# Streaming encoder layer on one core: the sample's high and low parts as one stationary block of 64 columns, logit rows of 544 and 640 columns cut in halves, row norms spread in three copies, rope tables written by GpSimd

## The chip, the cores and the metric

The kernel runs on one core of a Trainium2 chip. The metric is the device time of one execution in microseconds; the kernel before takes 1721.83 us in the median of three runs. The engines are TensorE (PE; its weight load is PEld), VectorE (DVE), ScalarE (ACT), GpSimd (POOL) and SyncE (SP), whose queue issues nearly all DMAs.

## What is computed

One layer over 1024 prompt tokens and 32 sample tokens, which share the weights; the sample also has 512 cached keys and values for each head. Cut to what matters here:

```python
z = einsum('bld,de->ble', rmsnorm(x, g_mix), w_in)        # q, k, v of A and B, indexer, gates
q_a, k_a = rope(rmsnorm(q_a, g_qn)), rope(rmsnorm(k_a, g_kn))
q_i, k_i = rope(q_i), rope(k_i)
score = einsum('bqhl,bqh->bql', relu(einsum('bqhd,bld->bqhl', q_i, k_i)), w_i)
_, idx = top_k(where(admissible, score, -inf), topk)      # 256 keys; for the sample 136 of 544
o_a = softmax over the selected keys of q_a k_a / 8, times v_a
o_b = stick-breaking weights of sigmoid(q_b k_b / 8), strictly causal, times v_b
h = x + (sigmoid(g_A) * (o_A @ W_bA) + sigmoid(g_B) * (o_B @ W_bB)) @ W_out
y = h + relu(rmsnorm(h) @ W_up)**2 @ W_down
```

All is float32 with float32 accuracy. For that, most operands are held as a high part and a low part (the names end in h and l), both in a rounded 32-bit format that TensorE multiplies fast, and a product is the sum of three: high times high, high times low and low times high.

## The kernel before

**Order.** The program is not issued as it is written. Every instruction is recorded by a planner (class Plan), which gives it a cost and a rank (FAST, PREP, MAIN, FILL, SLOW) and emits all engines' instructions in the order of its own simulated time. So each engine has one fixed order, and nearly all instructions carry the line of that emission, line 431. Tiles are named in the trace by what they hold, and in orders a number tells tiles of one name apart.

**Stages.** Index projection (0 to about 76 us), the spreading of the row norms (`spread_rs`), projection of mixer B with the index scores beside it, the top-k search by bits (until about 330 us), projection of mixer A (`project_a`, about 300 to 460), attention B (483 to 700), attention A (700 to 910), merge and feed-forward to the end.

**Sample rows.** Tokens are handled in nine blocks of rows: eight of 128, and block NEW of the 32 sample tokens. In `index_projection` (parts 0 and 1, 328 and 256 columns) and in `project_a` (four times, 256 columns) the tokens are TensorE's stationary operand (`xh`, `xl`) and the weights stream past. Each of eight slices of the inner dimension takes three matmuls. Block NEW takes as many as a full block: 24, with 32 stationary columns. The bank `s` or `pj` that they fill is then read by `ta` and `tb` on DVE, which rotate the rows with the rope tables `tabc` and `tabs`.

**Logit rows.** In `attend`, query block t has 128(t+1) keys, in pieces of at most 512 columns (`s<-k,q`, for the high and the low part of q). Block t = 4 has 640, cut into 512 and 128. `index_scores` cuts the same way (`s<-kih,qi`, `s<-kil,qi`), and the sample there has 512 cached and 32 new keys. `attend_new` computes the sample's 544 logits for four heads at a time, at four places of the program: for each head, two matmuls over the 512 cached keys `kc` (128 stationary columns, tile `qz`) and two over the 32 new keys `kn`. `kn` is loaded for four heads by one DMA; `kc` comes from the cache through `k<-ckb` or `k<-cka`, an ACT copy and a POOL subtraction, into a ring of three tiles that the keys `k` of `attend` and the new values `vn` use too.

**Small things.** `spread_rs` writes nine 128x128 tiles (`rsb`) on POOL, each a row norm spread over a row, and transposes them on TensorE. `rope_tables` makes `tabc` and `tabs` by four products on DVE at the start of `project_a`. The constants `tri`, `tri4` and a copy of the identity are made at the start of the program.

Of the kernel before, what the change touches and what calls it, by code (L numbers as in the profile page):

```python
# [21 lines left out]
KB = D // 128  # L22
# [22 lines left out]
GATES_BESIDE = (1,1,1,1,1,1,0,0)  # L45
# [9 lines left out]
def rows(s):  # L55

    return DEC if s == NEW else 128

# [392 lines left out]
class Layer:  # L451
# [74 lines left out]

    def x_of(self, k, cs):
# [7 lines left out]
    def run(self):  # L535
# [33 lines left out]
        self.ones = c([128, 128], F32, "ones")  # L569
        nc.vector.memset(self.ones, 1.0)  # L570
        self.ident = c([128, 128], F32, "ident")
        self.identr = c([128, 128], F32R, "identr")
        self.trir = c([128, 128], F32R, "trir")
# [13 lines left out]
        for i, n in enumerate((W1, T - W1)):  # L587
            self.xh.append(nc.tile(xp, [128, KB, n], F32R, f"xh{i}"))
            self.xl.append(nc.tile(xp, [128, KB, n], F32R, f"xl{i}"))
# [99 lines left out]
        self.ft = nc.tile(rp, [128, FWORDS], F32, "ft")  # L689
        self.turn = cycle(["pj", "a", "b", "c"])  # L690
# [11 lines left out]
    def constants(self):  # L702
        nc, a = self.nc, self.a
        for name, dst, n in (("tri", self.trir, 128), ("tri4", self.tri4r, DEC)):
            st = nc.tile(self.wpool, [128, 512], F32, name, tag="wst", bufs=3)
            nc.sync.dma_start(st[:, :n], a[name])
            nc.scalar.copy(dst, st[:, :n])
        nc.scalar.copy(self.identr, self.ident)
        nc.sync.dma_start(self.gf, a["g_ffn"])

    def normalise(self, sl):
# [4 lines left out]
        for hf in range(2):  # L716
# [7 lines left out]
            for kk in range(4):  # L724
# [36 lines left out]
    def index_setup(self):  # L761
# [9 lines left out]
        self.iw = [[None] * KB, None]  # L771

# [16 lines left out]
    def index_projection(self, part, s):  # L789
# [4 lines left out]
        if self.iw[part] is None:  # L794
# [7 lines left out]
            nc.scalar.copy(self.kih[:, T:], kc)  # L802
            nc.vector.tensor_sub(self.kil[:, T:], kc, self.kih.bitcast(F32)[:, T:])
# [4 lines left out]
        for k in range(KB):  # L808
            xh, xl = self.x_of(k, ts_)
            wh, wl = ws[k]  # L810
# [998 lines left out]
```

## Time and profile before

| | |
|---|---|
| median of three runs | 1721.83 us (1721.07 to 1722.91) |
| the profiled execution | 1724.92 us, of it the span of the profile 1723.0 us |
| mean granted TensorE clock | 0.997 |
| PE busy | 1691.1 us, 98% |
| DVE, ACT, POOL busy | 1346.7, 952.8, 854.2 us |
| share of the chain of work that ended last | PE 87%, DVE 6%, DMA 3% |

The profiled execution is one of its own, 0.2% above the median. Matmuls overlap: one of 272 columns has a duration of 0.29 us in the trace, while the next starts 0.125 us behind it. So what a matmul costs in a stream is read from the distance of starts. Where the timeline puts several into one row, the next row's start ends the last of them.

### The profile page before, as it was taken

Reading aid. Unit: us, or ns where it says so; the run is one execution under the profiler, and the core shown is the slowest. Engines: PE = TensorE matmul, PEld = TensorE weight load, DVE = VectorE, ACT = ScalarE, POOL = GpSimd, SP = SyncE. Lnnn points to the kernel's source line nnn. Section 1 sums busy time; section 2 is a strip of 40 time slices with the busy share of each in tenths; the row PEclk is TensorE's granted clock in tenths of the full one; section 3 lists DMA queues with packets and bytes.
Section 4 is the critical chain, followed back from the end, with each engine's and each line's share of the span. In section 5 each row is a group of like instructions: output and inputs, shape, how many; then the busy total and the mean of one; then the engine's idle time right before and its main releaser. Section 6 shows DMA issues by size and latency. Waiting matters only on the chain.

```text
span 1723.0 us, 34981 instructions
## 1 busy us (share of the span) xinstructions
PE 1691.1 (98%) x12356; PEld 1606.2 (93%) x12356; DVE 1346.7 (78%) x2773; ACT 952.8 (55%) x2023; POOL 854.2 (50%) x703
## 2 busy tenths in 40 slices
PE   7999999999999999999999999999999999999998
PEld 7988999899989899988999999999999999989998
DVE  8666899988568778775765648999988888797756
ACT  7455788765357768886655446333333444425431
POOL 5533331344367777365568757533333456556420
PEclk9999999999999999999999999999999999999999
DMA  7234453354673646686874643534443587756744
GB/s 255 82 100 126 128 161 116 89 151 139 172 207 101 172 103 173 177 243 190 243 213 148 179 135 116 165 135 152 136 153 132 189 286 245 266 169 232 255 127 149
DMA packets 182527, 289.08 MB, mean 168 GB/s; under 512 B 30800, under 2 KB 62128, under 8 KB 182352
## 3 DMA queue, kind: packets, MB, share of 16 engines
q1 hardware_dynamic: 182064, 286.50, 54.1%
q8 instruction: 98, 1.61, 0.4%
q14 instruction: 77, 0.63, 0.1%
q10 hardware_dynamic: 288, 0.34, 0.1%
HBM read 193.59 MB, written 93.07 MB: 166 GB/s over the span
## 4 chain that ended last, share of the span: by engine, by line
PE 87%; DVE 6%; DMA 3%; issue 1%; ACT 1%; POOL 1%; SPq 0%; DVEq 0%; ACTq 0%; POOLq 0%
PE pj L431 35%; PE s L431 11%; PE c L431 11%; PE b L431 10%; PE a L431 10%; PE t L431 5%; PE o L431 4%; DMA q<-dq 1%; DMA k<-cka 1%; DVE y L431 1%; DVE junk L431 1%; DVE us L431 1%; DVE mh L431 1%; DVE xl L431 1%; DMA xt<-x 0%
## 5 line engine op out<-in xcount | busy, mean ns | idle before, releaser
L431 POOL TENSOR_TENSOR wl<-wst,wh 128x512 fp32r<-128x512 f32 x160 | 229.5, 1440 | 231.0 <-ACT wh L431 172.3
L431 PE MATMUL pj<-xl,wh 128*128 128x272 f32 (+2 forms) x1200 | 336.4, 314 | 0.0
L431 PE MATMUL pj<-xh,wh 128*128 128x272 f32 (+1 forms) x768 | 253.3, 330 | 0.4 <-ACT sq L431 0.4
L431 PE MATMUL pj<-xh,wl 128*128 128x272 f32 (+1 forms) x768 | 252.6, 329 | 0.0
L431 PEld LDWEIGHTS pj<-xl,wh 128*128 128x128 f32 x1200 | 213.3, 189 | 11.4
L431 ACT CAST wh<-wst 128x512 fp32r<-128x512 f32 x213 | 131.1, 620 | 140.6 <-PE pj L431 23.4
L431 PEld LDWEIGHTS pj<-xh,wh 128*128 128x128 f32 x768 | 145.2, 189 | 11.5 <-ACT sq L431 0.7
L431 PEld LDWEIGHTS pj<-xh,wl 128*128 128x128 f32 x768 | 145.0, 189 | 10.5
L431 POOL TENSOR_TENSOR p<-p,rem 128x383 f32<-128x383 f32 (+8 forms) x66 | 110.7, 1697 | 31.8 <-DVE rem L431 25.1
L431 DVE TENSOR_TENSOR tt<-t,tt 128x512 fp32r<-128x512 f32 (+2 forms) x168 | 100.1, 620 | 33.2 <-ACT tt L431 32.7
L431 POOL TENSOR_TENSOR wl<-y,wh 128x512 fp32r<-128x512 f32 x49 | 72.9, 1490 | 96.1 <-ACT wh L431 93.0
L431 DVE TENSOR_TENSOR_SCAN rem<-rem 128x384 f32<-128x384 f32 (+8 forms) x66 | 110.6, 1696 | 9.7 <-ACT rem L431 9.6
L431 ACT CAST tt<-t 128x512 fp32r<-128x512 f32 (+2 forms) x168 | 85.8, 539 | 40.8 <-PE t L431 37.5
L431 ACT CAST wh<-y 128x512 fp32r<-128x512 f32 x79 | 49.1, 621 | 106.1 <-issue 23.0
L431 ACT CAST wh<-us 128x512 fp32r<-128x512 f32 x64 | 39.7, 622 | 114.6 <-PE pj L431 27.6
L431 PE MATMUL o<-tt,v 128*128 128x256 f32 (+1 forms) x640 | 99.0, 280 | 3.9 <-ACT tt L431 3.5
L431 ACT ACTIVATE junk<-score,cand 128x1024 bf16<-128x1024 f32 (+2 forms) x93 | 96.9, 1042 | 9.7 <-DVE cand L431 8.4
L431 PE MATMUL s<-k,q 128*128 128x512 f32 (+3 forms) x384 | 100.7, 357 | 1.3 <-DMA q<-dq 1.0
L431 PEld LDWEIGHTS o<-tt,v 128*128 128x128 f32 x640 | 91.8, 191 | 9.9 <-ACT tt L431 4.1
L431 DVE TENSOR_SCALAR_CACHE_REDUCE junk<-score,cand 128x384 bf16<-128x384 f32 (+1 forms) x124 | 92.9, 749 | 3.1
L431 PE MATMUL t<-ident,p 128*128 128x128 f32 (+1 forms) x596 | 91.0, 276 | 0.8 <-POOL p L431 0.6
L431 POOL TENSOR_TENSOR wl<-us,wh 128x512 fp32r<-128x512 f32 x33 | 50.3, 1533 | 71.3 <-ACT wh L431 71.3
(359 smaller groups left out, 5666.5 us busy)
## 6 DMA issues: line engine op xcount, KB each, us to landing
us<-w_down SPq DMA_DIRECT2D x80, 256.0 KB, 3.1
q<-dq SPq DMA_DIRECT2D x64, 256.0 KB, 4.9
du<-y SPq DMA_DIRECT2D x56, 264.0 KB, 2.5
du<-us SPq DMA_DIRECT2D x56, 264.0 KB, 2.5
y<-w_up SPq DMA_DIRECT2D x44, 256.0 KB, 2.7
k<-dk SPq DMA_DIRECT2D x40, 256.0 KB, 5.0
v<-dv SPq DMA_DIRECT2D x40, 256.0 KB, 4.4
xl<-du SPq DMA_DIRECT2D x35, 264.0 KB, 5.3
```

Source lines behind the costliest of these rows:

```text
L431: fn(*args, **kw)
```

## The change

1. `xh` of the second half of the tokens gets 32 more columns, filled by one ACT copy with the low parts of the sample. High and low parts so stand side by side as 64 stationary columns, and block NEW takes 16 matmuls in place of 24 (`token_rows`). The lower 32 rows of the result hold the low parts' products: one ACT copy and one DVE addition (`join`) add them to the upper rows, once in each of the six places.
2. Rows of 640 and 544 logits are cut into halves of 320 and 272 (`cut`). In `attend_new` the new keys stand behind the cached ones in the tile `kc`: 16 DMAs of 16 KB, one for each head, take the place of four for `kn`. The indexer's keys stand in the same order, the sample's cached ones ahead of its new ones.
3. `spread_rs` makes its tiles by three DVE copies in place of nine POOL instructions.
4. The four rope-table products go from DVE to POOL.
5. `tri`, `tri4` and the identity copy are made just ahead of attention B, and one gate is computed beside head 6 and not beside head 5.

```diff
-GATES_BESIDE = (1,1,1,1,1,1,0,0)
+GATES_BESIDE = (1,1,1,1,1,0,1,0)
...
+def cut(L):
+
+    return L // 2 if L in (640, LS) else 512
...
+    def token_rows(self, ps, s, ws):
+
+        mm = self.nc.tensor.matmul
+        if s == NEW:
+            for k in range(KB):
+                x = self.xh[1][:, k, SEQ - W1:]
+                for i in range(2):
+                    mm(ps[:2 * DEC], x, ws[k][i], start=k + i == 0, stop=k + i == KB)
+            return
+        for k in range(KB):
+            xh, xl = self.x_of(k, slice(128 * s, 128 * s + 128))
+            mm(ps, xh, ws[k][0], start=k == 0, stop=False)
+            mm(ps, xh, ws[k][1], start=False, stop=False)
+            mm(ps, xl, ws[k][0], start=False, stop=k == KB - 1)
+
+    def join(self, ps, low):
+
+        self.nc.scalar.copy(low, ps[DEC:2 * DEC])
+        self.nc.vector.tensor_add(ps[:DEC], ps[:DEC], low)
...
-            self.xh.append(nc.tile(xp, [128, KB, n], F32R, f"xh{i}"))
+            self.xh.append(nc.tile(xp, [128, KB, n + i * DEC], F32R, f"xh{i}"))
...
+        self.trir, self.identr = (nc.tile(self.att, [128, 128], F32R, z) for z in ("trir", "identr"))
+        nc.scalar.copy(self.identr, self.ident)
+        for name, dst, n in (("tri", self.trir, 128), ("tri4", self.tri4r, DEC)):
+            st = nc.tile(self.att, [128, 512], F32, name, tag="gz", bufs=3)
+            nc.sync.dma_start(st[:, :n], a[name])
+            nc.scalar.copy(dst, st[:, :n])
...
+        if sl[-1] == NEW:
+            nc.scalar.copy(self.xh[1][:, :, T - W1:], self.xl[1].bitcast(F32)[:, :, SEQ - W1:])
...
+            b = nc.tile(self.pr, [128, 2, 512], F32R, "rsb", tag="zz", bufs=2).bitcast(F32)[:, 0]
+            b = b.rearrange("p (t e) -> p t e", e=128)[:, :len(sl)]
+            nc.vector.tensor_copy(b, self.rs[:, sl[0]:sl[-1] + 1].unsqueeze(2).to_broadcast([128, len(sl), 128]))
             for i, s in enumerate(sl):
-                b = nc.tile(self.ip, [128, 5 * HD], F32, "rsb", tag="ta", bufs=2)[:, :128]
-                nc.gpsimd.tensor_scalar(b, self.ones, self.rs[:, s:s + 1], None, op0=ALU.mult)
                 m = rows(s)
-                nc.tensor.transpose(pt[:, i * 128:i * 128 + m], b[:m], self.ident[:m, :m])
+                nc.tensor.transpose(pt[:, i * 128:i * 128 + m], b[:m, i], self.ident[:m, :m])
...
-        for k in range(KB):
-            xh, xl = self.x_of(k, ts_)
-            wh, wl = ws[k]
-            nc.tensor.matmul(ps[:m, :n], xh, wh[:, :n], start=k == 0, stop=False)
-            nc.tensor.matmul(ps[:m, :n], xh, wl[:, :n], start=False, stop=False)
-            nc.tensor.matmul(ps[:m, :n], xl, wh[:, :n], start=False, stop=k == KB - 1)
+        self.token_rows(ps[:, :n], s, [[z[:, :n] for z in w] for w in ws])
+        if s == NEW:
+            self.join(ps[:, :n], nc.tile(self.wpool, [128, 512], F32, "pl", tag="wst", bufs=3)[:DEC, :n])
...
-        if t < 8:
-            L = 128 * (t + 1)
-            return [(c, min(512, L - c), c) for c in range(0, L, 512)]
-        return [(0, PAST, T), (PAST, DEC, SEQ)]
+        L = 128 * (t + 1) if t < 8 else LS
+        n = cut(L)
+        return [(c, min(n, L - c), c + (SEQ if t == 8 else 0)) for c in range(0, L, n)]
...
-            nc.vector.tensor_mul(self.tc_[:, :, j], C, g[:, j].unsqueeze(1).to_broadcast([128, NT, HD]))
+            nc.gpsimd.tensor_mul(self.tc_[:, :, j], C, g[:, j].unsqueeze(1).to_broadcast([128, NT, HD]))
...
+            self.token_rows(ps[:, :256], s, [
+                [u[:, i * 256:i * 256 + 256] for u in unit] for unit in units for i in range(2)])
+            if s == NEW:
+                self.join(ps[:, :256], nc.tile(pr, [128, 4, HD], F32, "pl", tag="sq", bufs=1).rearrange("p h e -> p (h e)")[:DEC])
...
-            for c0 in range(0, L, 512):
-                n = min(512, L - c0)
+            for c0 in range(0, L, cut(L)):
+                n = min(cut(L), L - c0)
...
-        kn = nc.tile(at, [128, 4, DEC], F32R, "kn", bufs=1)
-        nc.sync.dma_start(kn.bitcast(F32), self.dk[g0:g0 + 4, :, :, new].rearrange("j s e t -> (s e) j t"))
         for j in range(4):
             if j % 2 == 0:
                 k32 = nc.tile(at, [64, 2, PAST], F32, "k32", **(dict(tag="p", bufs=6) if is_a else dict(tag="rem", bufs=4)))
                 nc.sync.dma_start(k32, a["ck" + sfx][4 * u + j:4 * u + j + 2].rearrange("j e t -> e j t"))
-            k = nc.tile(at, [128, SEQ], F32R, "kc", tag="k", bufs=3)[:, :PAST]
-            nc.scalar.copy(k[:HD], k32[:, j % 2])
-            nc.gpsimd.tensor_sub(k[HD:], k32[:, j % 2], k.bitcast(F32)[:HD])
+            k = nc.tile(at, [128, SEQ], F32R, "kc", tag="k", bufs=3)[:, :LS]
+            nc.sync.dma_start(k.bitcast(F32)[:, PAST:], self.dk[g0 + j, :, :, new].rearrange("s e t -> (s e) t"))
+            nc.scalar.copy(k[:HD, :PAST], k32[:, j % 2])
+            nc.gpsimd.tensor_sub(k[HD:, :PAST], k32[:, j % 2], k.bitcast(F32)[:HD, :PAST])
             for i in range(2):
                 q, first, last = qq[:, i, 128 * j:128 * j + 128], j + i == 0, j + i == 4
-                nc.tensor.matmul(ps0, q, k, start=first, stop=last)
-                nc.tensor.matmul(ps1[:, :DEC], q, kn[:, j], start=first, stop=is_a and last)
+                nc.tensor.matmul(ps0[:, :LS // 2], q, k[:, :LS // 2], start=first, stop=last)
+                nc.tensor.matmul(ps1[:, :LS // 2], q, k[:, LS // 2:], start=first, stop=is_a and last)
...
-        parts = [(0, ps0[:, :]), (PAST, ps1[:, :DEC])]
+        parts = [(0, ps0[:, :LS // 2]), (LS // 2, ps1[:, :LS // 2])]
```

The planner lays the whole program out anew. Three places show it. The first is PE's order in the index projection, where block NEW's part 0 begins (`ih` and `il` are the high and low weights, `rr` and `kd` rotated rows to be transposed); before:

```order
L431 MATMUL s<-ih_128,xh_108 32x328
L431 MATMUL s<-il_129,xh_108 32x328
L431 MATMUL t<-ident,rr 128x128 x2
L431 MATMUL s<-ih_128,xl_109 32x328
L431 MATMUL s<-ih_130,xh_108 32x328
L431 MATMUL t<-ident,kd 128x128
L431 MATMUL s<-il_131,xh_108 32x328
L431 MATMUL s<-ih_130,xl_109 32x328
```

And on the same engine at the same place in the changed kernel:

```order
L436 MATMUL s<-ih_126,xh_105 64x328
L436 MATMUL s<-il_127,xh_105 64x328
L436 MATMUL s<-ih_128,xh_105 64x328
L436 MATMUL s<-il_129,xh_105 64x328
L436 MATMUL s<-ih_131,xh_105 64x328
L436 MATMUL s<-il_132,xh_105 64x328
```

The matmuls with `xl` are gone, and the result has 64 rows.

The second place is PE's order early in `project_a`, where the third part of the first values `vt` (32 columns at the end) is transposed, and further on the first rotated rows `qk`; before:

```order
L431 MATMUL pj<-xl_109,wh_1883 128x272
L431 MATMUL pj<-xh_108,wl_1884 128x272
L431 MATMUL t<-ident,vt 128x128 x2
L431 MATMUL t<-ident,vt 32x128
L431 MATMUL pj<-wh_1886,xh_108 128x256
...
L431 MATMUL pj<-wh_3889,xl_109 128x256
L431 MATMUL t<-ident,qk 128x128 x4
L431 MATMUL pj<-xh_106,wh_3946 128x512
```

The changed kernel's PE at that place:

```order
L436 MATMUL pj<-xl_106,wh_1802 128x272
L436 MATMUL pj<-xh_105,wl_1803 128x272
L436 MATMUL s<-wh_1805,xh_105 128x256
...
L436 MATMUL s<-wh_1808,xl_106 128x256
L436 MATMUL t<-ident,vt 128x128 x2
L436 MATMUL t<-ident,vt 32x128
L436 MATMUL pj<-wh_1805,xh_105 128x256
...
L436 MATMUL s<-wl_3872,xh_105 64x256
L436 MATMUL t<-ident,qk 128x128 x5
L436 MATMUL pj<-xh_103,wh_3929 128x512
```

Before, the transposes of `vt` stand directly behind the last matmul of their block, and those of `qk` 24 matmuls behind them. Now 12 matmuls of 256 columns stand ahead of the transposes of `vt`, and some 100 matmuls between them and those of `qk`.

The third place is SP's queue ahead of `attend_new` for the first four heads of mixer A; before:

```order
L431 DMA q<-dq 64x2x512 x2
L431 DMA wst<-w_bb 128x512
L431 DMA gz<-dg 128x512
L431 DMA kn<-dk 128x4x32
L431 DMA k_7444<-cka 64x2x512
L431 DMA k_7447<-cka 64x2x512
```

SP's queue there in the changed kernel:

```order
L436 DMA kc<-dk 128x32
L436 DMA q<-dq 64x2x512 x2
L436 DMA wst<-w_bb 128x512
L436 DMA gz<-dg 128x512
L436 DMA k_7397<-cka 64x2x512
L436 DMA k_7400<-cka 64x2x512
```

`kc<-dk` is the new keys' tail for one head. Three of four such DMAs are issued ahead of the cache's loads and one behind them, each into a tile of the ring of three.

## Rows read from the trace of the kernel before

**Rows 1.** The page: busy time of each engine, and the shares of the chain of work that ended last.

```profile
PE 1691.1 (98%) x12356; PEld 1606.2 (93%) x12356; DVE 1346.7 (78%) x2773; ACT 952.8 (55%) x2023; POOL 854.2 (50%) x703
PE 87%; DVE 6%; DMA 3%; issue 1%; ACT 1%; POOL 1%; SPq 0%; DVEq 0%; ACTq 0%; POOLq 0%
```

**Rows 2.** Windows: stretch and its length, then busy us (instructions) of PE, PEld, DVE, ACT and POOL, granted clock, DMA share, GB/s.

```profile
316.00:325.00 9.00, 4.78 (x38) 4.14 (x37) 8.48 (x32) 7.51 (x17) 4.38 (x4) 1.00 0.39 138
325.30:328.70 3.40, 3.40 (x10) 2.63 (x9) 2.84 (x8) 3.40 (x9) 1.89 (x2) 0.50 0.50 152
980.00:1723.00 743.00, 731.31 (x5819) 722.06 (x5818) 606.03 (x966) 298.09 (x606) 345.58 (x243) 1.00 0.54 179
```

**Rows 3.** PE's timeline, block NEW of the index projection: start, duration, matmul, stationary and moving shape. From the first row to the second 21 starts, from the third to the fourth 17.

```profile
61.97 0.28 PE L431 MATMUL s<-wl,xh 128*32 128x256 f32 x1
...
64.42 0.29 PE L431 MATMUL s<-wl,xh 128*32 128x256 f32 x1
...
73.78 0.31 PE L431 MATMUL s<-ih,xh 128*32 128x328 f32 x1
...
76.31 0.31 PE L431 MATMUL s<-ih,xl 128*32 128x328 f32 x1
```

**Rows 4.** PE's timeline beside the index scores: matmuls of 512, 128, 32 and 272 columns. From the first row of 272 to the last five starts.

```profile
130.25 0.39 PE L431 MATMUL pj<-xl,wh 128*128 128x512 f32 x1
130.47 0.22 PE L431 MATMUL s<-kih,qi 128*128 128x128 f32 x1
130.53 0.28 PE L431 MATMUL s<-kil,qi 128*128 128x128 f32 x1
130.65 0.45 PE L431 MATMUL pj<-xh,wl 128*128 128x512 f32 x1
...
131.64 0.26 PE L431 MATMUL s<-kih,qi 128*32 128x32 f32 x1
131.75 0.18 PE L431 MATMUL s<-kil,qi 128*32 128x32 f32 x1
131.78 0.48 PE L431 MATMUL pj<-xh,wl 128*128 128x512 f32 x1
...
138.87 0.29 PE L431 MATMUL pj<-xh,wh 128*128 128x272 f32 x1
...
139.50 0.29 PE L431 MATMUL pj<-xh,wl 128*128 128x272 f32 x1
```

**Rows 5.** PE's timeline in `attend_new`: eight matmuls over the new keys in one row and what follows, and two over the cached keys and what follows.

```profile
549.32 1.04 PE L431 MATMUL s<-kn,qz 128*128 128x32 f32 x8
550.21 0.26 PE L431 MATMUL s<-tri4r,identr 128*128 128x32 f32 x1
...
870.89 0.63 PE L431 MATMUL s<-kc,qz 128*128 128x512 f32 x2
871.36 0.49 PE L431 MATMUL t<-ident,p 128*128 128x128 f32 x3
```

**Rows 6.** PE's timeline at two waits in `project_a`; in brackets the idle time ahead and what ended it.

```profile
316.36 0.29 PE L431 MATMUL pj<-xh,wl 128*128 128x272 f32 x1
318.93 0.55 PE L431 MATMUL t<-ident,vt 128*128 128x128 f32 x3 [2.29 <-DVE vt L431]
...
322.04 0.28 PE L431 MATMUL pj<-wh,xl 128*128 128x256 f32 x1
323.83 0.63 PE L431 MATMUL t<-ident,qk 128*128 128x128 f32 x4 [1.52 <-DVE vs L431]
324.87 0.50 PE L431 MATMUL pj<-xh,wh 128*128 128x512 f32 x1 [0.42 <-ACT sq L431]
```

**Rows 7.** DVE's timeline there; `junk` counts scores for the top-k search.

```profile
317.75 0.77 DVE L431 TENSOR_SCALAR_CACHE_REDUCE junk<-score,cand 32x544 bf16<-32x544 f32 x1
318.45 0.07 DVE L431 DVE_READ_ACCUMULATOR junk<-score,cand 32x1 f32 x1
318.45 0.42 DVE L431 TENSOR_TENSOR vt<-pj,rb 128x272 f32<-128x272 f32 x1
...
322.94 0.74 DVE L431 TENSOR_TENSOR vs<-t,vs 128x256 fp32r<-128x256 f32 x2
323.61 0.40 DVE L431 TENSOR_TENSOR ta<-pj,tabc 128x256 f32<-128x256 f32 x1
```

**Rows 8.** Groups of instructions by shape: count, busy us and mean ns of one, idle time before; first DVE from 294 to 300 us, then POOL from 60 to 100 us; last POOL's timeline.

```profile
L431 DVE TENSOR_TENSOR tabc<-ropec,gqk 128x576 f32<-128x576 f32 x2 | 1.5, 741 | 0.0
...
L431 POOL TENSOR_SCALAR rsb<-ones,rs 128x128 f32<-128x128 f32 x9 | 5.4, 602 | 3.7 <-PE t L431 3.7
...
299.12 1.30 POOL L431 TENSOR_TENSOR wl<-wst,wh 128x512 fp32r<-128x512 f32 x1 [15.17 <-ACT wh L431]
```

**Rows 9.** The tile views of `kn` and then of `qz`: DMA issues on SP's queue (duration ns min/median/max), and the time from issue to landing.

```profile
L431 SPq DMA_DIRECT2D kn<-dk x4: 370/378/426, 493.0 to 795.3; - x4
DMA to landing us min/median/max: 2.8/4.9/8.5
...
L431 SPq DMA_DIRECT2D qz<-dq x16: 579/608/1095, 536.9 to 839.6; - x16
DMA to landing us min/median/max: 2.1/2.3/3.9
```

**Rows 10.** Waits from 795 to 811 us (total us, times, longest us).

```profile
ACT kc L431 <- DMA k<-cka: 3.6, 1, 3.6
PE o L431 <- ACT tt L431: 2.8, 1, 2.8
```

More of the change, by code (lines that the diff above doesn't have):

```diff
@@ L689, in run @@
         self.ft = nc.tile(rp, [128, FWORDS], F32, "ft")
+        self.ones = nc.tile(rp, [128, 128], F32, "sum")
+        nc.vector.memset(self.ones, 1.0)
         self.turn = cycle(["pj", "a", "b", "c"])
@@ L703, in constants @@
         nc, a = self.nc, self.a
[L704 to L708, printed above, removed]
         nc.sync.dma_start(self.gf, a["g_ffn"])
@@ L771, in index_setup @@
         self.iw = [[None] * KB, None]
+        self.ones = nc.tile(ik, [128, 128], F32, "ones")
+        nc.vector.memset(self.ones, 1.0)
     def index_weights(self, js):
@@ L801, in index_projection @@
                 nc.sync.dma_start(kc[HD * i:HD * i + HD], a["cki"])
-            nc.scalar.copy(self.kih[:, T:], kc)
-            nc.vector.tensor_sub(self.kil[:, T:], kc, self.kih.bitcast(F32)[:, T:])
+            old = slice(SEQ, SEQ + PAST)
+            nc.scalar.copy(self.kih[:, old], kc)
+            nc.vector.tensor_sub(self.kil[:, old], kc, self.kih.bitcast(F32)[:, old])
         ws = self.iw[part]
@@ L841, in index_projection @@
             nc.tensor.transpose(pk[:, :m], kd[:m].rearrange("p j e -> p (j e)"), self.ident[:m, :m])
-            nc.scalar.copy(self.kih[:, ts_], pk[:, :m])
-            nc.vector.tensor_sub(self.kil[:, ts_], pk[:, :m], self.kih.bitcast(F32)[:, ts_])
+            ks = slice(ts_.start + PAST * (s == NEW), ts_.stop + PAST * (s == NEW))
+            nc.scalar.copy(self.kih[:, ks], pk[:, :m])
+            nc.vector.tensor_sub(self.kil[:, ks], pk[:, :m], self.kih.bitcast(F32)[:, ks])
     def key_chunks(self, t):
-        if t < 8:
-            L = 128 * (t + 1)
-            return [(c, min(512, L - c), c) for c in range(0, L, 512)]
-        return [(0, PAST, T), (PAST, DEC, SEQ)]
+        L = 128 * (t + 1) if t < 8 else LS
+        n = cut(L)
+        return [(c, min(n, L - c), c + (SEQ if t == 8 else 0)) for c in range(0, L, n)]
     def index_scores(self):
@@ L952, in top_k @@
         nc, tp, tx, size = self.nc, self.top, self.top, self.size
-        minus = nc.tile(tp, [128, 1], F32, "minus")
+        minus, plus = (nc.tile(tp, [128, 1], F32, z) for z in ("minus", "plus"))
         nc.vector.memset(minus, -1.0)
+        nc.vector.memset(plus, 1.0)
         for g in self.groups:
@@ L988, in top_k @@
                     pre[:m, :L], pre[:m, :L], need[:m, j:j + 1], sgn[:m, :L], op0=ALU.is_ge, op1=ALU.subtract)
-                nc.scalar.activation(sq[:m, :L], pre[:m, :L], AF.Relu, bias=self.ones[:m, 0:1], scale=-1.0)
+                nc.scalar.activation(sq[:m, :L], pre[:m, :L], AF.Relu, bias=plus[:m], scale=-1.0)
                 nc.scalar.activation(self.mask[t][:m, :L], sq[:m, :L], AF.Copy, scale=NEG)
@@ L1074, in project_a @@
             m = rows(s)
-            ts_ = slice(128 * s, 128 * s + m)
             ps = self.bank(PA_BANKS[s % len(PA_BANKS)])
-            for k in range(KB):
-                xh, xl = self.x_of(k, ts_)
-                wh, wl = (u[:, (k % 2) * 256:(k % 2) * 256 + 256] for u in units[k // 2])
-                nc.tensor.matmul(ps[:m, :256], xh, wh, start=k == 0, stop=False)
-                nc.tensor.matmul(ps[:m, :256], xh, wl, start=False, stop=False)
-                nc.tensor.matmul(ps[:m, :256], xl, wh, start=False, stop=k == KB - 1)
+            self.token_rows(ps[:, :256], s, [
+                [u[:, i * 256:i * 256 + 256] for u in unit] for unit in units for i in range(2)])
+            if s == NEW:
+                self.join(ps[:, :256], nc.tile(pr, [128, 4, HD], F32, "pl", tag="sq", bufs=1).rearrange("p h e -> p (h e)")[:DEC])
             sq = nc.tile(pr, [128, 4, HD], F32, "sq", bufs=1)
@@ L1272, in attend_new @@
         else:
-            nc.tensor.matmul(ps1[:, :DEC], self.identr, self.tri4r, start=False, stop=True)
+            nc.tensor.matmul(ps1[:, LS // 2 - DEC:LS // 2], self.identr, self.tri4r, start=False, stop=True)
             p = self.stick_weights(parts, LS, *self.rooms(is_a))
```

6 lines of the change are left out of this document (1 added, 5 removed).

## The prediction

> **What bounds the kernel now.** The page comes first: PE is busy 98% of the span, and 87% of the chain that ended last is PE [rows 1]. So the kernel is a stream of matmuls, and what shortens the stream shortens the kernel, unless the time is lost again in a wait. The feed-forward part, 743 us long, has its order untouched by the change [rows 2]; all that can move lies before it. Second come PE's starts in the timeline, since a matmul costs the distance to the next start and not its duration [rows 3 to 5]. Third come the waits: PE stands for 2.29 us before the transposes of vt, until DVE has made them, and for 1.52 us before those of qk, until DVE has read vs [rows 6]. In the 9 us around both, PE is busy 4.78 us and DVE 8.48, so there DVE is the bound; behind them the granted clock is 0.50 for 3.4 us, which is the lower level of 1.2 GHz [rows 2]. That clock takes half of those 3.4 us from PE, 1.7 us.
>
> **The change part by part.** First what PE no longer does.
>
> Sample rows: 24 matmuls become 16, in eight slices. The stationary block has 64 columns in place of 32, the moving shape stays. With 256 columns a start follows the last by (64.42 - 61.97)/21 = 0.117 us, with 328 by (76.31 - 73.78)/17 = 0.149 [rows 3]. Full blocks of 128 stationary columns go at 0.125 for 272 columns [rows 4], so the width of the stationary block costs nothing there, and I take nothing for 64. Eight matmuls of 328 and five times eight of 256 go: 1.2 + 4.7 = 5.9 us.
>
> Rows of 640 logits: 512 and 128 columns become twice 320. 512 cost 0.235 (871.36 - 870.89, halved) [rows 5]; 128 cost 0.06 and 0.12 beside the index scores [rows 4]. 320 lie between 272 at 0.126 and 328 at 0.149, so 0.147. With 0.10 for the 128, a pair gives back 0.04 us. In attention there are 32 pairs: 1.2 us, with ends at 0 (0.06) and 1.7 (0.12). The index scores have 16 such pairs: 0.5 us.
>
> The sample's 544 columns: twice 272 is 0.25 us. Before, a pair in attend_new cost 0.235 for the cached keys and (550.21 - 549.32)/8 = 0.111 for the 32 new ones [rows 5]. So 0.096 goes in each of 32 pairs: 3.1 us. In the index scores the 32 columns cost 0.03 or 0.11 [rows 4]; with 0.05 over 16 pairs it is 0.5 us, between 0.2 and 1.5.
>
> The row says that 32 columns behind a block of 128 cost nearly what 256 do, and it measures the very matmuls that go. The Trainium skill ("TensorE: Matmul & The Clock Gate", section "Back-to-back issue gap") gives matmuls of up to 64 columns a floor of about 25 ns; by that the 3.1 would be an estimated 0.3 and the time 2.8 us later, which [rows 5] contradict.
>
> Together 5.9 + 1.2 + 0.5 + 3.1 + 0.5 = **11.2 us** of stream.
>
> Then the waits. The 2.45 us beyond the usual distance at vt (318.93 - 316.36 - 0.125) arise because the transposes stand directly behind their block, and vt comes late on DVE, behind a count of the top-k search at 317.75 [rows 6, 7]. In the new order of PE 12 matmuls stand between: 12 x 0.117 = 1.4 us of that wait is covered. The transposes of qk waited for vs, 1.52 us, 1.67 with what lies beyond the distance; now some 100 matmuls, over 10 us, stand ahead of them, and that wait goes. I take **3.1 us** for both. It could be more: the four rope tables leave DVE just ahead, 4 x 0.741 = 2.96 us [rows 8]. What is late next is ta and tb on DVE, which free the banks s and pj; five banks of 24 x 0.117 = 2.8 us each stand between. That DVE still has all counts of the search to do is the reason why I don't take the whole.
>
> What is added, and where it hides. The joins: an ACT copy and a DVE addition of 32 rows, some 0.4 us each (ta is 0.40) [rows 7], in six places. In the index projection the transposes that need them stand behind 26 matmuls of another bank, over 5 us; without that cover each costs 0.8 us, 4.8 in all. The rope tables on POOL: 512 columns take POOL 1.30 us, so 576 some 1.45, 5.8 in all; POOL had idled for 15.17 us there [rows 8]. If the first ta came before them, PE would find out only after its free banks, so nothing, up to 2 us. The nine spreading products, 5.4 us on POOL [rows 8], become three DVE copies of at most 512 columns, below vt's 0.42 for 272 doubled, 2 us together, at a place where PE has other blocks: nothing. The constants add two DMAs on SP's queue ahead of the keys and queries of attention B, at about 0.4 us each as for kn [rows 9]; gates fill PE there: nothing, up to 0.8.
>
> The 16 tails are the one addition that others queue behind. Their issues take 16 x 0.38 = 6.1 us in place of four, on a queue that is not PE's. But a tail waits in SP's queue until its tile of the ring of three is free, and every load and store behind it on SP waits too: q, the weights w_bb, the cache's keys (the third place of the order). ACT's copy of the cached keys waits for the same tile, as it did before. I take nothing for it, since the first three stand far ahead of their matmuls; the price if not is a rival.
>
> So the profiled execution's 1724.92 would become 1724.92 - 11.2 - 3.1 = 1710.6, its span 1708.7; against the median, 0.2% lower, 1721.83 - 14.3 = **1707.5 us**.
>
> **The rivals.**
> 1. *The stream shortens, the waits do not.* DVE is the bound around 316 us whatever PE's order is; what PE waits for there becomes a bank that ta and tb hold. For it speaks that DVE is busy 8.48 of 9 us [rows 2]. Then only 11.2 goes: 1710.6.
> 2. *All of that group goes.* DVE, freed of 2.96 us, is no longer late; the other 1.0 us of the vt wait goes, the 0.42 us for sq too, and the clock holds, 1.7: 1707.5 - 3.1 = 1704.4. Against it speaks that all of DVE's other work there remains, and the 8.48 of 9 us leave it little room.
> 3. *New waits in attention.* PE stood 2.8 us for tt there, because ACT's queue held a kc copy for the cache's keys for 3.6 us [rows 10]. The new order keeps kc copies ahead of tt. Such a wait in two more places, and in one the lower clock behind it for 1.7 us as in rows 2, take back 7.3: 1714.8. It can be more, up to no change.
> 4. *Slower: the tails hold SP's queue.* A DMA like kn's landed after 2.8 to 8.5 us, qz's after 2.1 to 3.9 [rows 9]. The tail of a place's fourth head waits for the first head's matmuls; between them and its own, the new order gives PE some 4 to 5 us by the distances above. Should each of 16 tails cost PE 14.3/16 = 0.9 us, the gain is gone; at 1.1 us it is 0.2% slower. At one landing of 8.5 against a cover of 4 in each place, with the next loads as late again, it is 4 x 4.5 + 4 x 1.5 = 24: about 1731.
> 5. *It does not do what it says.* With 64 stationary columns, which no row shows, a matmul could cost more than with 32: six blocks have 96 of them, and at 0.06 more each (0.18 for 256 columns) the 5.9 is gone: 1713.4. Blocks of 32 and of 128 stand at the same distance for their moving columns [rows 3, 4], which speaks against it. A smaller form: the new keys' 32 columns cost 0.111 in the run of eight shown, but 0.03 as at 131.75 in the other three places [rows 4, 5]: 24 x 0.08 = 1.9 us less gain, 1709.4.
>
> **How the numbers follow.** Forecast 0.38, rival 1 0.25, rival 2 0.10, rival 3 0.15, rival 4 0.08, rival 5 0.04. The likeliest is the forecast, 1707.5. About 0.2%, 3.4 us, is what a measurement of this kernel can tell from no change. Faster than 1718.4 are the forecast, rivals 1, 2 and 5 and half of rival 3: 0.85. Within the bound are the rest of rival 3 and a quarter of rival 4: 0.09. Slower: 0.06. The range reaches from 1703 (rival 2 with the upper ends of the pairs) to 1717 (rival 3 with the lower ends of the pairs, 2 us less); it leaves out a third of rival 2, half of rival 3 and rival 4, 0.19.
>
> **What would show it right or wrong.** PE's starts in block NEW at 0.117 and 0.149 with 16 matmuls; 0.125 for the 272 columns in attend_new; no matmul of 32 columns there. Around 310 to 330 us no wait of PE for vt above 1.3 us, none for vs. In attention, no wait of PE for kc, and tails that land before the cache's keys. Wrong would be: PE waiting for s or pj banks before 330 us (rival 1), for tt or kc (rivals 3 and 4), SP's queue standing at a tail with loads behind it (rival 4), or a start distance above 0.12 for 64 stationary columns (rival 5). The time from about 980 us on should be as long as before; if it is not, my bound to the first part was wrong.

## The result, and the profile after

The changed kernel takes 1711.89 us in the median of five runs (1710.22 to 1715.49), the kernel before 1721.76: a ratio of 0.9941, 95% interval 0.9929 to 0.9953, or 9.9 us between the medians (8.1 to 12.2 by the interval). The forecast was 1707.5, the range 1703 to 1717. Its profiled execution took 1715.49 us with a span of 1713.4; of the kernel before it was 1724.92 and 1723.0, so the two profiles stand 9.4 us apart. Each of the two is a long execution of its kernel: 1715.49 is the longest of the five, 3.6 us above their median, and 1724.92 lies 3.2 us above the median before.

The page after, its rows for the engines and for the chain:

```profile
PE 1681.0 (98%) x12308; PEld 1600.5 (93%) x12308; DVE 1349.4 (79%) x2780; ACT 953.0 (56%) x2028; POOL 839.7 (49%) x698
PE 82%; DVE 8%; DMA 5%; ACT 2%; issue 1%; POOL 1%; SPq 1%; DVEq 0%; ACTq 0%; POOLq 0%
```

Against [rows 1], PE is busy 10.1 us less, with 48 matmuls fewer. The stream is shorter, and on the chain, the sequence of work that ended last, DVE and DMAs have taken over 4 points from PE. PE's timeline shows that the stream is nearly as it was priced. First block NEW with 256 and with 328 columns, then the halves in attention and in attend_new:

```profile
61.74 0.28 PE L436 MATMUL s<-wl,xh 128*64 128x256 f32 x1
...
63.40 0.28 PE L436 MATMUL s<-wl,xh 128*64 128x256 f32 x1
...
71.38 0.31 PE L436 MATMUL s<-ih,xh 128*64 128x328 f32 x1
...
73.16 0.31 PE L436 MATMUL s<-ih,xh 128*64 128x328 f32 x1
...
566.77 0.80 PE L436 MATMUL s<-k,q 128*128 128x320 f32 x4
567.41 0.22 PE L436 MATMUL s<-trir,identr 128*128 128x128 f32 x1
...
870.84 0.41 PE L436 MATMUL s<-kc,qz 128*128 128x272 f32 x2
871.09 0.29 PE L436 MATMUL pj<-xl,wl 128*128 128x272 f32 x1
```

With 64 stationary columns 14 starts take 1.66 us, 0.119 each, and 12 take 1.78, 0.148: the distances of [rows 3]. Two halves of 272 take 0.25 us. Halves of 320 take 0.16 each here, a little more than the 0.147 assumed; with the forecast's other two prices a pair then gives back 0.015 us in place of 0.04, so the 1.2 us of that term would be some 0.5 (an estimate).

Windows of the changed kernel, columns as in [rows 2]: first the two around the old waits, then two with a lower clock, and the feed-forward part; last the one window of lower clock that the kernel before has in attention.

```profile
316.00:325.00 9.00, 8.84 (x54) 7.65 (x53) 8.69 (x29) 8.16 (x18) 5.13 (x5) 1.00 0.69 178
325.30:328.70 3.40, 3.40 (x31) 3.40 (x30) 3.30 (x14) 2.35 (x4) 0.79 (x2) 1.00 0.00 0
574.00:581.00 7.00, 6.71 (x37) 6.14 (x37) 6.42 (x7) 2.48 (x8) 7.00 (x4) 0.76 0.89 229
800.90:805.80 4.90, 4.90 (x26) 4.66 (x26) 1.57 (x3) 2.04 (x5) 4.74 (x4) 0.65 0.85 264
970.00:1713.00 743.00, 731.96 (x5824) 722.80 (x5822) 606.18 (x966) 298.71 (x607) 344.09 (x244) 1.00 0.54 180
...
806.50:809.90 3.40, 3.40 (x16) 3.10 (x15) 0.69 (x2) 1.20 (x3) 2.81 (x3) 0.51 0.79 236
```

The waits for vt and vs are gone with the lower clock behind them: PE is busy 8.84 of the 9 us where it was 4.78, while DVE is as busy as ever [rows 2, 6]. In attention there are two stretches of lower clock, each worth about 1.7 us (7.0 x 0.24 and 4.9 x 0.35), where the kernel before has one (3.4 x 0.49). The feed-forward part is as it was. Next PE's starts in attention, from its first logits to the first matmul behind it, of the kernel before and then of the changed one:

```profile
483.56 0.51 PE L431 MATMUL s<-k,q 128*128 128x384 f32 x2
...
932.74 0.41 PE L431 MATMUL a<-xl,wh 128*128 128x272 f32 x2
```

```profile
474.25 0.52 PE L436 MATMUL s<-k,q 128*128 128x384 f32 x2
...
923.25 0.41 PE L436 MATMUL a<-xl,wh 128*128 128x272 f32 x2
```

Attention begins 9.3 us earlier, and lasts 449.0 us where it lasted 449.2. So all of the gain lies ahead of it. There PE's waits of 0.2 us and more come to 12.0 us against 14.1, and the lower clock is gone, 1.7; some 5.5 us are left for the stream, priced at 6.9 ahead of attention. The 4.3 us of stream that the change takes out of attention bring 0.2. What took the rest is in the list of PE's waits there (changed kernel, 474 to 923 us; total us, times, longest us):

```profile
PE s L436 <- POOL kc L436: 2.7, 1, 2.7
PE s L436 <- DMA q<-dq: 1.8, 2, 1.2
PE o L436 <- POOL vcs L436: 1.1, 2, 0.8
PE pj L436 <- ACT wh L436: 1.1, 1, 1.1
PE o L436 <- DVE o L436: 0.9, 2, 0.5
```

With two small ones these are 8.2 us; the same list of the kernel before comes to 6.0, and it has one stretch of lower clock to the changed kernel's two. 2.2 and 1.7 us more account for 3.9 of the 4.1 that are missing in these two executions.

### The profile page after: what moved, and what is told of

Its sections match the earlier page's. It is cut to its first block, busy times and chain, and to the rows that moved or that the text cites. A ratio compares the mean times of both kernels' runs of the same rounds, so it can differ in the third digit from the quotient of the medians.

```text
span 1713.4 us, 34908 instructions
## 1 busy us (share of the span) xinstructions
PE 1681.0 (98%) x12308; PEld 1600.5 (93%) x12308; DVE 1349.4 (79%) x2780; ACT 953.0 (56%) x2028; POOL 839.7 (49%) x698
## 4 chain that ended last, share of the span: by engine, by line
PE 82%; DVE 8%; DMA 5%; ACT 2%; issue 1%; POOL 1%; SPq 1%; DVEq 0%; ACTq 0%; POOLq 0%
PE pj L436 33%; PE c L436 10%; PE b L436 10%; PE a L436 10%; PE s L436 10%; PE t L436 4%; PE o L436 4%; DVE junk L436 2%; DVE y L436 1%; DMA q<-dq 1%; SPq L436 1%; DMA k<-cka 1%; POOL vcs L436 0%; DVE us L436 0%; DMA xt<-x 0%
## 5 line engine op out<-in xcount | busy, mean ns | idle before, releaser
L436 POOL TENSOR_TENSOR wl<-wst,wh 128x512 fp32r<-128x512 f32 x160 | 225.6, 1417 | 193.9 <-ACT wh L436 186.5
L436 PEld LDWEIGHTS pj<-xh,wl 128*128 128x128 f32 x768 | 145.2, 189 | 10.2
L436 POOL TENSOR_TENSOR p<-p,rem 128x383 f32<-128x383 f32 (+8 forms) x66 | 99.4, 1520 | 52.8 <-DVE rem L436 32.0
L436 ACT ACTIVATE junk<-score,cand 128x1024 bf16<-128x1024 f32 (+2 forms) x93 | 97.0, 1043 | 12.4 <-DVE cand L436 10.8
L436 PE MATMUL s<-k,q 128*128 128x512 f32 (+4 forms) x384 | 99.1, 354 | 1.8 <-DMA q<-dq 1.8
```

The lines of the kernel that those rows point to most:

```text
L436: fn(*args, **kw)
```

## The experiments

Each was timed in five rounds against the kernel before, on more than one chip; so runs are best compared by the saving, each against the kernel before on the same chip. It is (1 - ratio) x 1722 us, with the interval's ends.

| run | median us | ratio (95% interval) | saving us |
|---|---|---|---|
| the change | 1711.89 | 0.9941 (0.9929 to 0.9953) | 10.2 (8.1 to 12.2) |
| f1_low_products | 1719.93 | 0.9983 (0.9972 to 0.9994) | 2.9 (1.0 to 4.8) |
| f2_new_keys | 1719.56 | 0.9986 (0.9976 to 0.9997) | 2.4 (0.5 to 4.1) |
| w_wide_cache | 1710.66 | 0.9939 (0.9925 to 0.9954) | 10.5 (7.9 to 12.9) |
| u_tables | 1715.68 | 0.9962 (0.9948 to 0.9976) | 6.5 (4.1 to 9.0) |
| u_rows | 1709.90 | 0.9924 (0.9911 to 0.9937) | 13.1 (10.8 to 15.3) |
| a_new | 1717.74 | 0.9972 (0.9962 to 0.9982) | 4.8 (3.1 to 6.5) |
| a_tables | 1717.56 | 0.9977 (0.9968 to 0.9986) | 4.0 (2.4 to 5.5) |
| w_keys_values | 1709.81 | 0.9924 (0.9911 to 0.9937) | 13.1 (10.8 to 15.3) |
| g_order_u_16 | 1715.30 | 0.9963 (0.9951 to 0.9975) | 6.4 (4.3 to 8.4) |
| h_order_after_24 | 1714.08 | 0.9960 (0.9949 to 0.9972) | 6.9 (4.8 to 8.8) |
| g_wide_cache | 1715.40 | 0.9958 (0.9942 to 0.9973) | 7.2 (4.6 to 10.0) |
| u_rows_keys_values | 1715.92 | 0.9971 (0.9961 to 0.9981) | 5.0 (3.3 to 6.7) |

**One thing left out, the order kept.** The emission skips the matmuls marked here (the same is done in `project_a`); the planner and all queues are as before.

```diff
...
+            nc.leave = s == NEW
             nc.tensor.matmul(ps[:m, :n], xl, wh[:, :n], start=False, stop=k == KB - 1)
+            nc.leave = False
...
```

> The order of the kernel before, word for word, but the 48 matmuls that multiply the sample's low parts in block NEW are left out (8 of 328 columns, 40 of 256), and nothing is joined; so the sample's projections lack that product. Theory (the change gains by the columns that TensorE no longer streams, and the waits sum up the same): 8 x 0.149 + 40 x 0.117 = 5.9 us go, 1721.8 becomes 1715.9. Rival (DVE sets the pace until 325 us, so what TensorE saves before that is lost in a longer wait for vt): the index projection's 2.1 us and the first of project_a's four blocks, 0.9, come back as wait, 2.9 us go, 1718.9.

2.9 us, at most 4.8: the rival's number, and the 5.9 are excluded. Attention's first logits and PE's longer waits in the profile of this run:

```profile
316.13 0.55 PE L435 MATMUL t<-ident,vt 128*128 128x128 f32 x3 [3.23 <-DVE vt L435]
...
477.41 0.56 PE L435 MATMUL s<-k,q 128*128 128x384 f32 x2
...
486.34 1.05 PE L435 MATMUL s<-k,q 128*128 128x512 f32 x4 [1.56 <-DMA q<-dq]
...
802.14 0.39 PE L435 MATMUL o<-tt,v 128*128 128x256 f32 x1 [3.85 <-ACT tt L435]
```

The wait for vt is 0.94 us longer than in [rows 6], the one for tt 1.1 longer than in [rows 10], and one for q at attention's start is new. The rival had only the first of them: part of what PE saves is waited for wherever a slower engine or a load is due, not only where DVE is the bound. How large a part, the profile does not tell: in it the lower clock of [rows 2] is missing too, attention begins 6.2 us earlier, and the execution is 5.1 us shorter than the profiled one before. The 2.9 rest on the timed executions.

In the second run:

```diff
...
+                nc.leave = not first and not last
                 nc.tensor.matmul(ps1[:, :DEC], q, kn[:, j], start=first, stop=is_a and last)
+                nc.leave = False
...
```

> The order of the kernel before, but 24 of the 32 matmuls of 32 columns over the sample's new keys are left out (the first and the last of each group of eight stay), so the sample's logits for its new keys are not whole. Theory (such a matmul costs 0.111 us behind a block of 128 stationary columns, as in the rows): 24 x 0.111 = 2.7 us go, 1719.1. Rival (a short matmul costs 0.03 us, as behind a long one): 0.7 us go, 1721.1.

2.4 us, near the 2.7 of 0.111 us each; but the interval, 0.5 to 4.1, holds the rival's 0.7 too, so the time leans to the price of [rows 5] and does not settle it. PE's timeline of this run does, at the place of [rows 5]:

```profile
548.75 0.37 PE L435 MATMUL s<-kn,qz 128*128 128x32 f32 x2
548.98 0.26 PE L435 MATMUL s<-tri4r,identr 128*128 128x32 f32 x1
```

Two take 0.23 us where eight took 0.89, so each of the six that are gone took 0.11. At the other three places the kernel before has 0.09 to 0.11 each; the rival's 0.03 is out.

**Tables.** Two runs, one undoing the part, one doing it alone:

```diff
...
-            nc.gpsimd.tensor_mul(self.tc_[:, :, j], C, g[:, j].unsqueeze(1).to_broadcast([128, NT, HD]))
+            nc.vector.tensor_mul(self.tc_[:, :, j], C, g[:, j].unsqueeze(1).to_broadcast([128, NT, HD]))
...
```

> The changed kernel with its four rope tables back on DVE; the planner lays it out anew, mostly around 290 to 330 us. Theory (the group of waits at 316 to 329 us went because the new order puts other matmuls ahead of the transposes): no wait for vt above 1 us, the time within 1 us of 1711.9. Rival (it went because DVE was freed of 2.96 us there): the waits for vt and vs come back, with the lower clock behind them, 3 to 6 us, 1715 to 1718.

3.7 us come back by the savings, though the two intervals touch, and waits come with them: one for vt, and one for tb in place of vs (PE's timeline of this run):

```profile
314.14 0.55 PE L436 MATMUL t<-ident,vt 128*128 128x128 f32 x3 [1.61 <-DVE vt L436]
...
319.55 0.47 PE L436 MATMUL pj<-xh,wh 128*128 128x512 f32 x1 [1.36 <-DVE tb L436]
```

The clock does not fall behind them here.

> The kernel before with one part of the change alone: the four rope tables on GpSimd. TensorE's work is untouched. Theory (DVE being freed of 2.96 us is what ends the waits for vt and vs at 316 to 325 us and the lower clock behind them): about 3.6 us go, as much as came back when the tables went back to DVE in the changed kernel, 1718.1. Rival (the waits go only together with the shorter stream of the sample rows): within 1 us of 1721.7.

4.0 us go, and the window of the old waits is full, in this kernel whose matmuls are all those of before:

```profile
316.00:325.00 9.00, 9.00 (x63) 8.02 (x61) 8.31 (x31) 8.17 (x16) 5.61 (x6) 1.00 0.24 63
```

So the tables' move ends that group. The planner answers it by putting matmuls ahead of the transposes of vt, in both kernels that have the move and in neither that has not. It also puts those transposes earlier: at 302.9 us in the changed kernel and 302.7 in a_tables, where they stood at 318.9 before and stand at 314.1 in u_tables. The tables themselves were on DVE from 295 to 298 us, 20 us ahead of the late vt, so what their move changed there is at least in part the layout. How much is DVE's relief and how much PE's order cannot be told apart by these runs.

**New keys alone.**

```diff
...
-                nc.tensor.matmul(ps0, q, k, start=first, stop=last)
-                nc.tensor.matmul(ps1[:, :DEC], q, kn[:, j], start=first, stop=is_a and last)
+                nc.tensor.matmul(ps0[:, :LS // 2], q, k[:, :LS // 2], start=first, stop=last)
+                nc.tensor.matmul(ps1[:, :LS // 2], q, k[:, LS // 2:], start=first, stop=is_a and last)
...
```

> The kernel before with one part of the change alone: the sample's 544 logits in two halves of 272, with the new keys as tails of the cached ones in 16 DMAs. Theory (32 matmuls of 32 columns at 0.111 us go, and the tails are hidden): 3.0 us go, 1718.7. Rival (the tails hold SP's queue, or attention waits for loads whatever TensorE saves): no change, 1721.7, or slower by more than 1 us, with waits of TensorE or ACT for a tail.

4.8 us (3.1 to 6.5), the theory's 3.0 just below the interval, and no wait of PE for a tail; the rival is out. In this layout PE also lost its 2.8 us wait for tt in attention A, for which the theory had no term.

**Sample rows undone.**

```diff
         if s == NEW:
-            for k in range(KB):
-                x = self.xh[1][:, k, SEQ - W1:]
-                for i in range(2):
-                    mm(ps[:2 * DEC], x, ws[k][i], start=k + i == 0, stop=k + i == KB)
-            return
+            ps = ps[:DEC]
         for k in range(KB):
-            xh, xl = self.x_of(k, slice(128 * s, 128 * s + 128))
+            xh, xl = self.x_of(k, slice(128 * s, 128 * s + rows(s)))
...
-        if s == NEW:
-            self.join(ps[:, :n], nc.tile(self.wpool, [128, 512], F32, "pl", tag="wst", bufs=3)[:DEC, :n])
```

> The changed kernel with block NEW of the sample back at 24 matmuls of 32 stationary columns, without the joins; everything else of the change stays, and the planner lays all out anew. Theory (the 64 columns give what the stream loses, since the re-laid order lets the rest follow): 5.9 us come back, 1717.8. Rival (as in the run with the low products left out, about half of what TensorE saves here is lost in waits anyway): 3 us come back, 1714.9.

Both were wrong: with 5.9 us of stream put back the kernel is no slower, 2 us faster by the median, with intervals that overlap. Its attention:

```profile
480.14 0.34 PE L436 MATMUL s<-k,q 128*128 128x384 f32 x1
...
918.16 0.42 PE L436 MATMUL a<-xl,wh 128*128 128x272 f32 x2
```

It begins 5.9 us later than in the changed kernel, the price of the rows to a tenth; that it fits so well is luck, since a stretch of lower clock at 75 to 79 us (1.7 us), which the changed kernel's profile has not, is in it. It lasts 438.0 us, 11.0 less. PE's waits there come to 1.2 us against 8.2, and no stretch has a lower clock: 7.0 + 3.4 = 10.4 of the 11.0.

The 11.0 are those of one execution. By the medians the new layout gives 2.0 us more than the rows cost it, so 7.9 if these cost their whole 5.9, and 4 to 5 if they cost the 2 to 3 of the runs that keep the order. And one of the two stretches of lower clock does not belong to the layout: in w_wide_cache, below, the same matmuls run in the same order at 574 to 581 us, behind the same wait for vcs (0.28 us), and the clock stays up:

```profile
574.00:581.00 7.00, 6.72 (x48) 6.21 (x48) 6.65 (x8) 3.34 (x10) 7.00 (x4) 1.00 0.90 244
```

**A table of two orders by two counts.** Here the planner sees one kernel and the emission writes the other: in the order of u_rows 16 matmuls and the joins (the diff; `wide` emits a matmul with 64 stationary columns, `none` emits nothing), in the changed kernel's order, by the same means, 24 matmuls and no join.

```diff
...
         fn, args, kw = n.call
+        if n.emit is not None:
+            fn = n.emit(fn)
...
+            self.nc.emit = wide(0) if s == NEW else None
             mm(ps, xh, ws[k][0], start=k == 0, stop=False)
+            self.nc.emit = wide(1) if s == NEW else None
             mm(ps, xh, ws[k][1], start=False, stop=False)
+            self.nc.emit = none if s == NEW else None
             mm(ps, xl, ws[k][0], start=False, stop=k == KB - 1)
...
```

> The order of the run u_rows kept on every engine, but block NEW's 24 matmuls are emitted as 16 with 64 stationary columns, each join (an ACT copy, a DVE addition) just ahead of the first reader of its bank, and the copy of the low parts behind the last of them. Theory (the 5.9 us of stream are real, and the changed kernel lost them again because the planner laid its attention out worse): attention starts 5.9 us earlier than in u_rows and stays as short, 1709.9 becomes 1704.0. Rival (what TensorE saves ahead of attention is waited for there, because loads and not TensorE set attention's pace): 1708 to 1710, with new waits between 475 and 920 us.

> The order of the changed kernel kept on every engine, but block NEW is emitted as 24 matmuls of 32 stationary columns, and the six joins are left out, which are not needed then. With the run before it, this makes a table of two orders by 16 or 24 matmuls. Theory (the waits in attention belong to the order): the waits at 575 and 798 us stay, 5.9 us come back, 1711.9 becomes 1717.8. Rival (the waits come from TensorE being early for its loads): they shrink by what TensorE arrives later, and 1712 to 1714 results.

| median us (saving us) | 24 matmuls | 16 matmuls |
|---|---|---|
| order of u_rows | 1709.90 (13.1) | 1715.30 (6.4) |
| order of the changed kernel | 1714.08 (6.9) | 1711.89 (10.2) |

Each order has its better median with the count that it was laid out for; in the second row the intervals of the two savings overlap. For g_order_u_16 both forecasts failed, 1704.0 and 1708 to 1710. Its attention stays short (439.3 us by the starts), as the theory said, but begins at 482.04 us, 1.9 later than in u_rows and not 5.9 earlier. PE's waits between 20 and 482 us come to 8.7 us against 3.4 in u_rows, and the clock falls twice before 90 us where it falls once there: 5.3 + 1.7 = 7.0 of the 7.8 us. First the timeline and a window of u_rows, then of this run:

```profile
74.25 0.44 PE L436 MATMUL t<-ident,rr 128*128 128x128 f32 x2 [1.62 <-POOL rr L436]
...
72.00:90.00 18.00, 16.27 (x81) 11.59 (x79) 10.14 (x43) 6.64 (x18) 7.45 (x12) 0.91 0.17 48
```

```profile
75.65 0.44 PE L440 MATMUL t<-ident,rr 128*128 128x128 f32 x2 [2.32 <-POOL rr L440]
84.79 0.28 PE L440 MATMUL t<-ident,rr 32*128 32x32 f32 x2 [1.28 <-POOL mask L440]
...
72.00:90.00 18.00, 14.29 (x62) 11.15 (x62) 10.35 (x39) 6.25 (x17) 7.45 (x13) 0.81 0.23 61
```

The wait for a full block's rotated rows (128x128) is in both. New is the one for the sample's own rows (32x32), whose transposes stand where 24 matmuls had covered them and 16 with a join do not (read from the order, not tried by itself), and the second stretch of lower clock behind it. The executions of this run took 1709.25 to 1719.41 us, the profiled one 1718.04. So that run does not show what 5.9 us ahead of u_rows' attention would do. In the second, PE's starts in attention and its longest wait are:

```profile
478.66 0.52 PE L440 MATMUL s<-k,q 128*128 128x384 f32 x2
...
801.14 0.40 PE L440 MATMUL s<-kc,qz 128*128 128x272 f32 x1 [1.41 <-POOL kc L440]
...
921.99 0.41 PE L440 MATMUL a<-xl,wh 128*128 128x272 f32 x2
```

Attention begins 4.4 us later and lasts 443.3 us, 5.7 less than with 16; the wait for kc is 1.41 us in place of 2.66, without the lower clock behind it. The rival holds, 1714.08 at the upper end of its 1712 to 1714: part of the waits came from PE being early. By the medians the rows are worth 2.2 us in this order, by the savings 3.3. The two profiles do not show it: the one with 24 matmuls is 1.3 us shorter.

**Later loads made earlier.**

```diff
...
-                nc.sync.dma_start(k32, a["ck" + sfx][4 * u + j:4 * u + j + 2].rearrange("j e t -> e j t"))
+                nc.sync.dma_start(k32, a["ck" + sfx][4 * u + j:4 * u + j + 2].rearrange("j e t -> (j e) t"))
...
```

> The changed kernel in the same order on all engines, but the cached keys of two heads are loaded over 128 partitions (128x512) in place of 64 (64x2x512); high and low parts change places for every second head. The bytes stay. Theory (the wait of 2.66 us for kc at 798 us and the lower clock behind it come from the landing of two narrow loads, 9.7 us after their issue, where loads of the same size over 128 partitions land in 4.6): the wait goes, and 1.7 us of clock with it, 1711.9 becomes about 1707.4. Rival (the landing is late because SP's queue and the DMA engines are full there, so the shape changes nothing): 1711.9, with the wait as long as now.

The time did not move beyond the intervals. The keys are there 7.3 us after their issue (785.28, by SP's timeline) in place of 9.8 (789.03), and the wait for kc is gone; the next load in ACT's queue, the cached values, has taken its place. ACT's timeline and PE's, of the changed kernel and then of this run:

```profile
798.79 1.77 ACT L436 CAST kc<-k 64x512 fp32r<-64x512 f32 x3 [4.99 <-DMA k<-cka]
...
800.86 0.39 PE L436 MATMUL s<-kc,qz 128*128 128x272 f32 x1 [2.66 <-POOL kc L436]
```

```profile
792.55 1.91 ACT L436 CAST kc<-k 64x512 fp32r<-64x512 f32 x3 [2.02 <-DMA k<-cka]
...
800.82 0.40 ACT L436 CAST vcs<-vc 128x256 fp32r<-128x256 f32 x1 [2.95 <-DMA vc<-cva]
...
801.89 0.39 PE L436 MATMUL o<-tt,v 128*128 128x256 f32 x1 [2.08 <-ACT tt L436]
```

With the values in the same tiles, right behind the keys:

```diff
...
+                vc = k32[:, PAST:].rearrange("p (j k e) -> p j k e", j=2, k=4)
+                k32 = k32[:, :PAST]
...
+                nc.sync.dma_start(vc, a["cv" + sfx][4 * u + j:4 * u + j + 2].rearrange("j p k e -> p j k e"))
...
-                vc = nc.tile(at, [128, 2, 4, HD], F32, "vc", tag="o", bufs=2)
-                nc.sync.dma_start(vc, a["cv" + sfx][4 * u + j:4 * u + j + 2].rearrange("j p k e -> p j k e"))
...
```

> The changed kernel with the cached keys loaded over 128 partitions and the cached values in the second half of the same tiles, issued right behind the keys; their own ring, which they shared with the outputs o, falls away. The planner lays attention out anew. Theory (TensorE's long wait in attention A is a chain of late loads, keys first, values next, and both are now early): no wait above 1.5 us between 780 and 820 us, no lower clock there, 1711.9 becomes about 1707.5. Rival (another late load or an ACT copy takes their place, as the values did for the keys): 1710 to 1712.

PE waits nowhere between 780 and 820 us now, where it is busy all of the 40 us at the full clock, and 1709.81 lies 2 us below the change, less than the 4.4 that the theory had; the two intervals overlap. The last two runs put this together with others.

> The run g_order_u_16 with the cached keys loaded over 128 partitions besides, the order unchanged but for those DMAs' neighbours on SP. Theory (in this order no wait hangs on the cache's loads): the same as that run within 1.5 us. Rival (the narrow loads still cost something in attention A): 2 to 3 us less than that run.

The same as g_order_u_16, as the theory had it: no wait there hung on these loads.

> Two versions that each came out 2 us below the changed kernel put together: block NEW back at 24 matmuls without joins, and the cached keys and values loaded wide into one tile. The planner lays it out anew. Theory (TensorE's stream is 5.9 us longer, but attention has no late load left): about 1708, with attention (from its first logits to the feed-forward part) near 438 us. Rival (each gain was a layout's, and the next layout has its own waits): 1710 to 1714, with attention above 441 us.

The rival in kind, and beyond it in size: 1715.92, above its 1710 to 1714 and slower than either alone. Attention has a wait of its own in the new layout and lasts 445.4 us; PE's waits there come to 6.0 us:

```profile
478.21 0.52 PE L436 MATMUL s<-k,q 128*128 128x384 f32 x2
...
626.84 0.50 PE L436 MATMUL s<-k,q 128*128 128x256 f32 x2 [2.16 <-ACT p L436]
...
923.62 0.41 PE L436 MATMUL a<-xl,wh 128*128 128x272 f32 x2
```

The best versions run are u_rows and w_keys_values, at 1709.9 and 1709.8; they beat the kernel before clearly, and the changed kernel only by what the intervals leave open.

## Why the prediction was right, and where it was off

The direction, the range and the bound were right: PE's stream sets the pace, the kernel is faster by part of what leaves it, and the feed-forward part is as long as before. The forecast was 4.4 us too low. By the number rival 1, 1710.6, came nearer; by the mechanism it is out, since the waits that it kept are gone.

- *The prices in the stream held.* 0.119 and 0.148 for 64 stationary columns, 0.25 for two halves of 272; of the rows' 5.9 us, 4.4 show at attention's start when the order is kept (h_order_after_24). That they were prices of the stream and not of the kernel is the step that failed. "Together 11.2 us of stream" went into the time whole, and the rows' 5.9 were worth 2 to 3 us where the order was kept (2.2 by the medians of h_order_after_24; 2.9 in f1_low_products, 1.0 to 4.8): PE comes earlier, and vt, q, kc and tt do not, or not as much. A smaller slip is in the sum itself: 32 pairs at 0.04 are 1.3 us and not 1.2, and their upper end is 2.0 and not 1.7.
- *The waits at 316 us.* I took 3.1 of them. The tables' move alone gives 4.0, and undoing it costs 3.7, so the size was near, by luck in part: I had put the tables' relief of DVE into "it could be more" and PE's order first, and the runs show that without the tables' move there is no such order.
- *What is late next.* I named the banks that ta and tb free; what came was attention, rival 3: 2.2 us more of waits, among them the 2.66 for kc that I had named as a sign of being wrong, and one more stretch of lower clock, 3.9 us against the 7.3 of its price. The stretch is not the layout's doing alone, as w_wide_cache shows. I gave it 0.15 as if it were a case of its own. It is a part of every case, since all of attention was laid out anew.
- *The tails (rival 4)* cost PE nothing that the profile shows but one weight load's wait of 0.3 us, and a_new, which has all 16, gained 4.8 us. The joins measured 0.36 and 0.41 us, the tables on POOL 1.44 each, as estimated; that the joins need matmuls behind them to hide, which the forecast had said, g_order_u_16 bears out where it took that cover away.
- *What stays open.* The parts measured singly, 4.0 for the tables, 4.8 for the halves of 272 and 2.2 to 2.9 for the rows, come to 11 to 12, near the measured 9.9; but each interval is some 3 us wide, and each of the first two carries the luck of its own layout, so the sum proves little. The halves of 320, the spreading by DVE, the moved constants and the gate were not run alone. Why one layout of attention has 1.2 us of waits and another 8.2 was followed to the loads and copies named, not to a rule that would tell it ahead.

## What to carry to other kernels

Where one engine is busy 98% of the time, a shorter stream on it is worth its price only as far as the loads and the other engines' results come earlier too; in an order that stays as it was, about half arrived here (2.9 of 5.9 us, between 1.0 and 4.8). Where a planner lays everything out anew, the change of layout is a term of the sum with a size of its own, here 438 to 449 us for the same attention in single executions, and 4 to 8 us by the medians of two layouts, and it belongs in every case's range. A run that keeps the order and leaves the matmuls out separates the two, as long as nothing in the order counted on the time that they took. One profiled execution is one sample: where it stands among the timed ones is to be looked at before its waits are added up.

## What the runs showed of the hardware that had not been expected

- The clock fell to its lower level (0.50 from 577 to 580 us) in the changed kernel though PE was recorded busy for 16.7 of the 17 us ahead, with matmuls of 64 columns among others and one wait of 0.29 us for vcs. In w_wide_cache PE did the same there, 16.7 of 17 us with a wait of 0.28, and the clock stayed at 1.00. So what PE is recorded to do ahead did not decide it: of two executions of the same stretch, one lost 1.7 us.
- A matmul of 32 columns costs 0.111 us behind a stationary block of 128 columns [rows 5] and mostly 0.03 behind one of 32 (131.75 to 131.78 in [rows 4]; 0.11 at 131.64, behind three transposes): in a row of short ones the stationary block sets the pace.
- 512 KB of cached keys were usable 9.8 us after their issue when loaded over 64 partitions, and 7.3 us over 128, with the same bytes. Over the four loads of mixer A's cached keys the median from issue to landing was 7.5 and 5.5 us, over mixer B's 4.8 and 4.0.
- Executions of one kernel spread by 0.4%: the kernel before took 1718.6 to 1726.1 us over 18 executions on one chip. A difference of 2 us needs many of them.
